# A decoder layer on one core: the first norm's first four blocks turned by VectorE and DRAM transfers, the first pooling group placed later

## The chip, the cores and the metric

The kernel runs on one core of a Trainium2 chip. The metric is the device time of one execution in microseconds (us), lower is better. Three executions of the kernel before took 984.05, 984.94 and 985.39 us (median 984.94). The engines are named as in the profile: PE is TensorE, DVE VectorE, ACT ScalarE, POOL GpSimd, SP the engine that mostly issues transfers.

## The reference

The kernel computes one layer of a decoder for 1024 tokens of width 1024 in float32.

```python
z = h @ w_in[i]                                  # 1024 -> 512 pool | 512 q | 128 k | 128 v
y_pool = pool_mixer(u_pool, w_pool[i], pool_scale[i])   # causal means over 2, 4, 8, 16 tokens, minus the token, one 128x128 map per group
y_attn = sliding_window_attention(q, k, v, attn_sinks[i])  # 8 query heads, 2 kv heads, band of 128, sinks
mix = jnp.concatenate([y_pool, y_attn], axis=-1) @ w_out[i]
h = layer_norm(DEEPNORM_ALPHA * h + mix, ln1_g[i], ln1_b[i])
ff = jnp.square(jax.nn.relu(h @ w_ff1[i])) @ w_ff2[i]      # 1024 -> 4096 -> 1024
h = layer_norm(DEEPNORM_ALPHA * h + ff, ln2_g[i], ln2_b[i])
gate = jax.nn.sigmoid(h @ w_ple_gate[i] + b_ple_gate[i])
h = h + gate * (p[i] @ w_ple[i])
```

## The kernel before, in words

The 1024 tokens are eight blocks of 128; a block is called a token here, as in the code (`n` from 0 to 7), and four of them make a half (`t` = 0 or 1, 512 tokens). Every float32 product is made of three matmuls: each operand is split into a high part (a cast, `high`, L101, on ACT) and the rest (a subtraction, `low`, L106, on DVE or POOL), and `mm3` (L116 to L118) issues high·high, high·low, low·high into one PSUM bank.

The kernel is written as a plain sequence of calls. A scheduler that simulates the engines turns it into one fixed order of instructions for each engine and its queue; each engine then works through its order and waits, where an operand or a buffer is not ready, with everything behind it. So a call that is moved in the text can change the order on all engines for some distance around it. Buffers come from pools by tag, each with a small number of slots: in PSUM the tag `s` has two banks (attention scores, L298 and L299, and the fourth accumulator of `out_left`), `av` one, and further banks hold `pt` (transposes) and `mm` (accumulators).

The stages around the change:

- Projection and attention. `z_tile` makes 128 columns of z for one half (24 matmuls). `attention(n)` makes the scores of a query block in tiles `s`, four per block, two score pairs in each; DVE empties them (L302, into `e`), ACT takes the exponential (L309), DVE scales (L313, L315), PE transposes `e` (L322), ACT and DVE split it (`pp`), and PE multiplies with the values (L327, L328, `av`).
- Pooling. `pool_group(gi, t, o)` (L354 to L388) takes the z tile `o` of one of four groups: ACT copies it (L358), POOL builds the window sums (L366), DVE subtracts (L369), ACT and DVE split the result into `tmp`, PE multiplies with the group's map (`mm<-tmp,wp`), and ACT and DVE scale and split that (L385). There are eight groups, in the order of `steps`, and `pooling(n)` keeps two z tiles ahead of them.
- Mixing. `out_left(t)` makes the left 512 columns of the output projection for four tokens at once, `out_right(n)` the right 512 for one token; `residual` (L457, DVE) adds them onto the input block `hn[n]` and thereby frees the PSUM bank.
- First norm. `norm1(n)` normalises `hn[n]` (L404 to L424 and L121: statistics and two long passes on DVE, one on ACT, one short step on POOL), turns it so that the columns lie on the partitions (`transposed`, L444: eight 128x128 PE transposes per token, four into a bank of tag `pt` and four into `av`), scales the unturned block and stores it (L549, L550, ACT), and splits the two turned halves into X["11"] and X["21"] (ACT casts, DVE subtractions); for tokens 0 to 2 the first is also copied into `pre` (L553).
- The feed-forward stage begins with `early(p)` (L598 to L612), which loads a piece of w_ff1 on SP's queue (L600), splits it, and multiplies it with X["11"] and X["21"] of the first half. In the text the order is out_right(0..3), out_left(1), norm1(0..3), residual of tokens 4 to 7, out_right(4..7), early(0).
- In the tail a similar turning is already done without PE: `flip` (L427 to L436) has DVE transpose 32x32 blocks of a token, writes the result to a DRAM scratch `td` (512 KB) and reads it back in four pieces of 128 KB with the blocks rearranged, all on POOL's queue.

Of the kernel before, what the change touches and what calls it, by code (L numbers as in the profile page):

```python
# [7 lines left out]
F32 = mybir.dt.float32  # L8
# [4 lines left out]
P = 128  # L13
D = 1024
S = 1024
HALF = 512
NT = S // P
NK = D // P
# [52 lines left out]
def layer(ctx, tc, xT, x, pT, w_in, w_pool, pscale, sinks, w_out, ln1, w1, w2, ln2, w_ple, w_gate, bgate, bias, rcount, out):  # L71
# [63 lines left out]


    h_dram = [tc.dram_tile([P, D], F32, name=f"hd{n}") for n in range(NT)]
    t_dram = [tc.dram_tile([P, 4, 2 * P], F32, name=f"td{n}") for n in range(2 * NT)]
    s_dram = [tc.dram_tile([P, 2, HALF], F32, name=f"sd{q}") for q in range(NSUM)]
    g_dram = {t: [tc.dram_tile([P, 2, HALF], F32, name=f"g{t}{i}") for i in range(2)] for t in ("T1", "T2", "T3", "T4")}  # L140
    f_dram = [tc.dram_tile([P, 2, 2, 2, HALF], F32, name=f"fd{q}") for q in range(NQUAD - NKEEP)]
# [32 lines left out]
    def tr_ps():  # L174
        return ps.tile([P, 4, P], F32, tag="pt", bufs=2, name=nm("pt"))
# [15 lines left out]
    def z_tile(c, t, home=None):  # L191
        w = (home or wt)([P, 2, NK, P])
        loads.append(load_split(w[:, 0], w[:, 1], w_in[c], [P, NK, P], nc.vector))
        o = acc_ps()
        for k in range(NK):
            z_mm(o, w, t, k)
        return o
# [146 lines left out]
    steps = [(gi, t) for t in range(2) for gi in (3, 2, 1, 0)]  # L344
    ahead = []

    def pooling(n):
        for _ in range(n):
            while steps and len(ahead) < 2:
                gi, t = steps.pop(0)  # L350
                ahead.append((gi, t, z_tile(6 + gi, t)))
            pool_group(*ahead.pop(0))

    def pool_group(gi, t, o):  # L354
        win = WINDOWS[gi]
# [82 lines left out]
    def tr_av():  # L438
        return ps.tile([P, 4, P], F32, tag="av", bufs=1, name=nm("av"))

    def transposed(y, j, pt):
        for k in range(4):
            kt = 4 * j + k
            nc.tensor.transpose(pt[:, k, :], y[:, kt * P : (kt + 1) * P], ident)  # L444
        return pt
# [54 lines left out]
    keys(1, z_tile(0, 1))  # L500
    attention(2)
    queries(1, 1)
    pooling(1)
    attention(3)
    values(1, z_tile(1, 1))
    pooling(1)
    attention(4)
    pooling(2)
    attention(5)
    pooling(2)  # L510
    attention(6)
    pooling(2)
    left = out_left(0, lambda: stage([P, 2, HALF]), nc.vector)
    with tc.issue_after(loads[-1].ins):
        residual_load(0)
# [10 lines left out]
    def part(shape=(P, 2, 4, P), dt=F32R):  # L526
        return p1.tile(list(shape), dt, tag="ws", bufs=6, name=nm("ws"))
# [10 lines left out]
    def split_to(name, c, src, eng):  # L538
# [2 lines left out]
        high(dh, src)  # L541
        return low(eng, X[name][:, 1, :, cs], src, dh)

    def norm1(n):
        t, c = n // 4, n % 4
        layer_norm(hn[n], gb1)
        a = transposed(hn[n], 0, tr_ps())
        b = transposed(hn[n], 1, tr_av())
        nc.scalar.mul(out=hn[n], in_=hn[n], mul=ALPHA)  # L549
        nc.scalar.dma_start(out=h_dram[n], in_=hn[n])  # L550
        if t == 0:
# [603 lines left out]
```

## Time and profile before

| what | value |
|---|---|
| median of three executions | 984.94 us |
| profiled execution | 984.01 us, its span 982.2 us |
| granted TensorE clock | 1.000 |
| PE busy | 973.8 us, 99% |
| DVE busy | 750.4 us, 76% |
| ACT busy | 470.6 us, 48% |
| POOL busy | 129.5 us, 13% |
| mean DMA rate | 175 GB/s |

The profile is of one execution; its times count from the first instruction, and the execution's own time is longer than this span by 1.8 us. A row of the timeline gives start, duration, engine, line, operation and tiles, and in brackets how long the engine was idle before it and what ended that. A row of the chain gives start, the time that the piece holds the path, engine, tile and line. A row of waits gives who waited for whom, the sum in us, how often, and the longest. Successive matmuls overlap, so a duration of a matmul is longer than its share of the path. PE idles at few places: at the start, at 92.8 and 156.6 us in the attention phase, and in the tail.

### The profile page before, as it was taken

To read this page: it belongs to the slowest core of one execution; us is meant where nothing else is said; L and a number is where in the kernel's file an instruction comes from. 1 tells how busy PE (TensorE), PEld (TensorE's weight loads), DVE (VectorE), ACT (ScalarE), POOL (GpSimd) and SP (SyncE) were. 2 spreads that over 40 slices of the span, in tenths; PEclk is the share of its full clock that TensorE was granted. 3 is DMA by queue.
4 is the path that set the end of the run, shared out by engine and by line. 5 is a ranking of instruction groups with operands and counts; after the bars stand their busy time and mean duration, and the time that the engine had idled before them with its cause. 6 is when DMAs were issued, how large, how long until landed. Compare 5 with 4: busy or idle time off the path is not lost.

```text
span 982.2 us, 12301 instructions
## 1 busy us (share of the span) xinstructions
PE 973.8 (99%) x4474; PEld 809.3 (82%) x4474; DVE 750.4 (76%) x1188; ACT 470.6 (48%) x749; POOL 129.5 (13%) x185
## 2 busy tenths in 40 slices
PE   9999999999999999999999999999999999999998
PEld 7888887888888888888888888888888888878887
DVE  5798888895868876867547666888657699799895
ACT  5676666543475443434444344443434354554341
POOL 0013552020010000110000000100011111203210
PEclk9999999999999999999999999999999999999999
DMA  6512142623152544896264794675788866762741
GB/s 220 183 65 86 44 150 75 219 82 115 69 198 103 197 150 159 298 324 242 78 245 172 278 322 149 150 243 194 207 217 190 223 158 225 252 193 77 257 148 55
DMA packets 48188, 172.13 MB, mean 175 GB/s; under 512 B 6016, under 2 KB 7168, under 8 KB 45312
## 3 DMA queue, kind: packets, MB, share of 16 engines
q1 hardware_dynamic: 35584, 130.05, 38.6%
q0 software_dynamic: 10960, 36.71, 14.6%
q10 hardware_dynamic: 1584, 4.59, 1.2%
q8 instruction: 35, 0.57, 0.2%
q14 instruction: 25, 0.20, 0.1%
HBM read 138.82 MB, written 32.51 MB: 174 GB/s over the span
## 4 chain that ended last, share of the span: by engine, by line
PE 94%; DVE 2%; DMA 2%; issue 1%; ACT 1%; DVEq 0%
PE f L117 21%; PE f L118 21%; PE f L116 21%; PE mm L116 8%; PE mm L118 8%; PE mm L117 8%; DMA ws<-in_w_gate 2%; PE pt L322 1%; PE s L299 1%; PE s L298 1%; PE av L328 1%; PE av L327 1%; DVE w L106 0%; PE s L116 0%; ACT c L101 0%
## 5 line engine op out<-in xcount | busy, mean ns | idle before, releaser
L117 PE MATMUL f<-x,w 128*128 128x512 f32 x448 | 174.0, 389 | 0.4 <-DVE x L106 0.4
L118 PE MATMUL f<-x,w 128*128 128x512 f32 x448 | 173.9, 389 | 0.0
L116 PE MATMUL f<-c,ws 128*128 128x512 f32 (+1 forms) x420 | 162.5, 387 | 0.0
L117 PE MATMUL f<-c,ws 128*128 128x512 f32 (+1 forms) x420 | 162.5, 387 | 0.0
L118 PE MATMUL f<-c,ws 128*128 128x512 f32 (+1 forms) x420 | 161.3, 387 | 0.0
L116 PE MATMUL f<-x,w 128*128 128x512 f32 x448 | 147.1, 389 | 0.1
L101 ACT CAST w<-st 128x1024 fp32r<-128x1024 f32 (+2 forms) x66 | 65.6, 999 | 100.2 <-issue 57.9
L106 DVE TENSOR_TENSOR w<-st,w 128x1024 fp32r<-128x1024 f32 (+2 forms) x66 | 77.5, 1177 | 46.9 <-ACT w L101 46.8
L117 PEld LDWEIGHTS f<-x,w 128*128 128x128 f32 x448 | 84.1, 188 | 18.8 <-DVE x L106 1.1
L116 PEld LDWEIGHTS f<-x,w 128*128 128x128 f32 x448 | 84.0, 188 | 17.9 <-ACT x L101 0.5
L118 PEld LDWEIGHTS f<-x,w 128*128 128x128 f32 x448 | 84.1, 188 | 17.3
L118 PEld LDWEIGHTS f<-c,ws 128*128 128x128 f32 x420 | 78.9, 188 | 16.5 <-DVE ws L106 0.4
L117 PEld LDWEIGHTS f<-c,ws 128*128 128x128 f32 x420 | 78.9, 188 | 16.0
L116 PEld LDWEIGHTS f<-c,ws 128*128 128x128 f32 x420 | 78.9, 188 | 16.0
L106 DVE TENSOR_TENSOR x<-ws,x 128x1024 fp32r<-128x1024 f32 x54 | 65.8, 1219 | 1.5 <-ACT x L101 1.5
L101 ACT CAST ws<-w 128x512 fp32r<-128x512 f32 x60 | 36.9, 622 | 52.0 <-PE f L118 26.5
L106 DVE TENSOR_TENSOR ws<-w,ws 128x512 fp32r<-128x512 f32 x60 | 41.2, 690 | 25.3 <-ACT ws L101 24.6
L101 ACT CAST x<-ws 128x1024 fp32r<-128x1024 f32 x54 | 56.6, 1048 | 7.4 <-DMA ws<-gT 4.0
L101 ACT CAST ws<-st 128x512 fp32r<-128x512 f32 x48 | 29.8, 620 | 62.2 <-DVE st L121 30.8
L116 PE MATMUL mm<-c,w 128*128 128x512 f32 x144 | 56.4, 396 | 0.3 <-ACT w L101 0.3
L118 PE MATMUL mm<-c,w 128*128 128x512 f32 x144 | 56.6, 394 | 0.0
L117 PE MATMUL mm<-c,w 128*128 128x512 f32 x144 | 56.4, 393 | 0.0
(236 smaller groups left out, 1905.5 us busy)
## 6 DMA issues: line engine op xcount, KB each, us to landing
ws<-in_w SPq DMA_DIRECT2D x70, 512.0 KB, 3.8
w<-in_w SPq DMA_DIRECT2D x16, 1024.0 KB, 5.4
c<-fd SPq DMA_DIRECT2D x6, 2048.0 KB, 8.6
fd<-n POOLq DMA_DIRECT2D x20, 512.0 KB, 4.3
ws<-in_w POOLq DMA_DIRECT2D x20, 512.0 KB, 7.6
st<-in_w_in SPq DMA_DIRECT2D x17, 512.0 KB, 3.4
ws<-in_w_gate SPq DMA_DIRECT2D x16, 512.0 KB, 4.6
w<-in_w SPq DMA_DIRECT2D x10, 512.0 KB, 4.0
```

What stands on the lines that cost most here:

```text
L101: nc.scalar.copy(out=dst, in_=src)
L106: return eng.tensor_tensor(out=dst, in0=src, in1=hi.bitcast(F32), op=ALU.subtract)
L116: nc.tensor.matmul(o, ah, bh, start=first, stop=False, skip_group_check=more)
L117: nc.tensor.matmul(o, ah, bl, start=False, stop=False, skip_group_check=more)
L118: nc.tensor.matmul(o, al, bh, start=False, stop=last, skip_group_check=more)
L298: nc.tensor.matmul(s[:, i, dst], ql, kt[:, 0, g, kk : kk + kn], start=True, stop=False)
L299: nc.tensor.matmul(s[:, i, dst], ql, kt[:, 1, g, kk : kk + kn], start=False, stop=True)
L322: nc.tensor.transpose(pt[:, i, :], e[:, i, kb * P : (kb + 1) * P], ident)
L327: nc.tensor.matmul(av, VV[0][:, blk, g], pp[:, 0], start=(kb == lo), stop=False)
L328: nc.tensor.matmul(av, VV[0][:, blk, g], pp[:, 1], start=False, stop=(kb == 1))
```

## The change

There are two parts. The first pooling group (`gi` 3 of half 0), whose z tile is still made behind `queries(1, 1)`, is worked off only behind attention(3) and the z tile of the second half's values; `pooling` is replaced by `project` (make the next z tile) and direct calls of `pool_group`, and the sequence of all later calls stays what it was. And for tokens 0 to 3 `norm1` no longer has PE transposes: `flip_first` has DVE transpose 32x32 blocks of the normalised token into two rows of `pre`, SP writes them to the token's DRAM scratch and reads four pieces back into a tile of tag `ws`, and ACT and DVE make the same copies and splits as before out of that tile in SBUF. Tokens 4 to 7 keep the PE transposes. The argument `False` of `layer_norm` is its default.

```diff
--- before.py
+++ after.py
@@ -135,7 +135,7 @@
 
 
     h_dram = [tc.dram_tile([P, D], F32, name=f"hd{n}") for n in range(NT)]
-    t_dram = [tc.dram_tile([P, 4, 2 * P], F32, name=f"td{n}") for n in range(2 * NT)]
+    t_dram = [tc.dram_tile([4, P, 2 * P] if n < 4 else [P, 4, 2 * P], F32, name=f"td{n}") for n in range(2 * NT)]
     s_dram = [tc.dram_tile([P, 2, HALF], F32, name=f"sd{q}") for q in range(NSUM)]
     g_dram = {t: [tc.dram_tile([P, 2, HALF], F32, name=f"g{t}{i}") for i in range(2)] for t in ("T1", "T2", "T3", "T4")}
     f_dram = [tc.dram_tile([P, 2, 2, 2, HALF], F32, name=f"fd{q}") for q in range(NQUAD - NKEEP)]
@@ -344,12 +344,9 @@
     steps = [(gi, t) for t in range(2) for gi in (3, 2, 1, 0)]
     ahead = []
 
-    def pooling(n):
-        for _ in range(n):
-            while steps and len(ahead) < 2:
-                gi, t = steps.pop(0)
-                ahead.append((gi, t, z_tile(6 + gi, t)))
-            pool_group(*ahead.pop(0))
+    def project():
+        gi, t = steps.pop(0)
+        ahead.append((gi, t, z_tile(6 + gi, t)))
 
     def pool_group(gi, t, o):
         win = WINDOWS[gi]
@@ -500,16 +497,28 @@
     keys(1, z_tile(0, 1))
     attention(2)
     queries(1, 1)
-    pooling(1)
+    project()
+    project()
     attention(3)
-    values(1, z_tile(1, 1))
-    pooling(1)
+    zv = z_tile(1, 1)
+    pool_group(*ahead.pop(0))
+    values(1, zv)
+    project()
+    pool_group(*ahead.pop(0))
     attention(4)
-    pooling(2)
+    project()
+    pool_group(*ahead.pop(0))
+    project()
+    pool_group(*ahead.pop(0))
     attention(5)
-    pooling(2)
+    project()
+    pool_group(*ahead.pop(0))
+    project()
+    pool_group(*ahead.pop(0))
     attention(6)
-    pooling(2)
+    project()
+    pool_group(*ahead.pop(0))
+    pool_group(*ahead.pop(0))
     left = out_left(0, lambda: stage([P, 2, HALF]), nc.vector)
     with tc.issue_after(loads[-1].ins):
         residual_load(0)
@@ -541,11 +550,29 @@
         high(dh, src)
         return low(eng, X[name][:, 1, :, cs], src, dh)
 
+    def flip_first(y, n, t):
+        b, d = pre[:, 2 * (n % 2) : 2 * (n % 2) + 2].rearrange("p a b -> p (a b)"), t_dram[n]
+        nc.vector.transpose(
+            out=b.rearrange("p (q k c) -> p q k c", q=4, k=NK),
+            in_=y.rearrange("p (k q r) -> p q k r", k=NK, q=4),
+        )
+        nc.sync.dma_start(out=d.rearrange("q p e -> p q e"), in_=b.rearrange("p (q e) -> p q e", q=4))
+        for q in range(4):
+            nc.sync.dma_start(
+                out=t[32 * q : 32 * q + 32].rearrange("r (R e) -> r R e", R=4),
+                in_=d[q].rearrange("(R r) e -> r R e", R=4),
+            )
+        tv = t.rearrange("p (R k c) -> p k R c", R=4, k=NK)
+        return tv[:, 0:4], tv[:, 4:8]
+
     def norm1(n):
         t, c = n // 4, n % 4
-        layer_norm(hn[n], gb1)
-        a = transposed(hn[n], 0, tr_ps())
-        b = transposed(hn[n], 1, tr_av())
+        layer_norm(hn[n], gb1, False)
+        if t == 0:
+            a, b = flip_first(hn[n], n, part((P, D), F32))
+        else:
+            a = transposed(hn[n], 0, tr_ps())
+            b = transposed(hn[n], 1, tr_av())
         nc.scalar.mul(out=hn[n], in_=hn[n], mul=ALPHA)
         nc.scalar.dma_start(out=h_dram[n], in_=hn[n])
         if t == 0:
```

The scheduler's order changes at three places that matter here. The first is PE between the end of `out_left(1)` (tile s_342) and `out_right(4)`. Before (pt and av are the transposes of tokens 0 and 1, mm_369 is the accumulator of out_right(4)):

```order
L116 MATMUL s_342_2144<-x7_338_2140,c_197_1303 128x512
L117 MATMUL s_342_2144<-x7_338_2140,c_197_1303 128x512
L118 MATMUL s_342_2144<-x7_338_2140,c_197_1303 128x512
L444 MATMUL pt_355_2281<-ident_61,n_298_1892 128x128 x4
L444 MATMUL av_356_2286<-ident_61,n_298_1892 128x128 x4
L444 MATMUL pt_359_2312<-ident_61,n_299_1894 128x128 x4
L116 MATMUL mm_369_2394<-c_323_2011,c_243_1555 128x512
L117 MATMUL mm_369_2394<-c_323_2011,c_243_1555 128x512
L118 MATMUL mm_369_2394<-c_323_2011,c_243_1555 128x512
```

And after (mm_365 is the accumulator of out_right(4)):

```order
L116 MATMUL s_342_2144<-x7_338_2140,c_197_1303 128x512
L117 MATMUL s_342_2144<-x7_338_2140,c_197_1303 128x512
L118 MATMUL s_342_2144<-x7_338_2140,c_197_1303 128x512
L116 MATMUL mm_365_2382<-c_323_2011,c_243_1555 128x512
L117 MATMUL mm_365_2382<-c_323_2011,c_243_1555 128x512
L118 MATMUL mm_365_2382<-c_323_2011,c_243_1555 128x512
```

Three groups of transposes are gone between the two; the other five, which stood among the products of out_right(4..7), are gone as well.

The second place is DVE from there back to the norm. Before (n_301 is token 3, normalised, n_349 and n_350 are tokens 4 and 5, ws and w are splits of the weights of early(p), sm are small statistics):

```order
L106 TENSOR_TENSOR ws_379_2505<-ws_378_2503,ws_379_2505 128x512
L106 TENSOR_TENSOR ws_380_2508<-ws_378_2503,ws_380_2508 128x512
L419 SCALAR_TENSOR_TENSOR sm_366_2363<-sm_366_2363 128x1
L106 TENSOR_TENSOR ws_390_2568<-ws_389_2566,ws_390_2568 128x512
L106 TENSOR_TENSOR ws_391_2571<-ws_389_2566,ws_391_2571 128x512
L420 TENSOR_SCALAR sm_366_2363<-sm_366_2363 128x1
L421 TENSOR_TENSOR sm_366_2363<-sm_366_2363 128x1
L424 SCALAR_TENSOR_TENSOR n_301_1898<-n_301_1898,sm_366_2363,st_329_2029 128x1024
L106 TENSOR_TENSOR ws_395_2606<-w_394_2604,ws_395_2606 128x512
L106 TENSOR_TENSOR ws_396_2609<-w_394_2604,ws_396_2609 128x512
L121 TENSOR_TENSOR n_301_1898<-n_301_1898,st_330_2030 128x1024
L457 SCALAR_TENSOR_TENSOR n_349_2259<-n_349_2259,mm_339_2141 128x512
```

And after (pre is what the block transposes write, n_300 is token 2, ws_355 and ws_358 are tokens 0 and 1 as they come back from DRAM, c_335 and c_336 are X["11"] and X["21"]; L421 and L454 are the lines that were L424 and L457):

```order
L106 TENSOR_TENSOR c_335_2137<-ws_355_2281,c_335_2137 128x4x128
L106 TENSOR_TENSOR c_336_2138<-ws_355_2281,c_336_2138 128x4x128
L121 TENSOR_TENSOR n_300_1896<-n_300_1896,st_330_2030 128x1024
L417 TENSOR_SCALAR sm_363_2354<-sm_363_2354 128x1
L555 STREAM_TRANSPOSE pre_337_2139<-n_300_1896 128x1024
L418 TENSOR_TENSOR sm_363_2354<-sm_363_2354 128x1
L421 SCALAR_TENSOR_TENSOR n_301_1898<-n_301_1898,sm_363_2354,st_329_2029 128x1024
L121 TENSOR_TENSOR n_301_1898<-n_301_1898,st_330_2030 128x1024
L555 STREAM_TRANSPOSE pre_337_2139<-n_301_1898 128x1024
L106 TENSOR_TENSOR c_335_2137<-ws_358_2309,c_335_2137 128x4x128
L106 TENSOR_TENSOR c_336_2138<-ws_358_2309,c_336_2138 128x4x128
L454 SCALAR_TENSOR_TENSOR n_349_2259<-n_349_2259,mm_339_2141 128x512
```

The weight splits have left this stretch for one behind it; four block transposes (L555, two of them in these rows) and the low parts of tokens 0 and 1 have come into it, ahead of the residual that frees the bank of mm_339. On SP's queue the four reads of token 1 stand behind a load of `w` for the early products, which is issued when its slot is free, and all transfers of the flips stand ahead of the first two loads (`ws`) of early(0) and early(1), which were ahead of the norm before.

The third place is PE ahead of `out_left(0)`, late in the attention phase. Before (pt and e belong to an attention block, s_266 is a score tile, mm_280 the product of a pooling group, s_289 the fourth accumulator of out_left(0)):

```order
L322 MATMUL pt_230_1483<-ident_61,e_225_1456 128x128
L322 MATMUL pt_232_1493<-ident_61,e_225_1456 128x128 x4
L298 MATMUL s_266_1666<-k_100_726,n_129_903 128x256
L299 MATMUL s_266_1666<-k_100_726,n_129_903 128x256
L116 MATMUL mm_280_1750<-tmp_279_1747,wp_122 128x512
L117 MATMUL mm_280_1750<-tmp_279_1747,wp_122 128x512
L118 MATMUL mm_280_1750<-tmp_279_1747,wp_122 128x512
L116 MATMUL s_289_1775<-w_290_1776,c_141_988 128x512
L117 MATMUL s_289_1775<-w_290_1776,c_141_988 128x512
```

And after (mm_275 is a z tile, the dots stand for six more of its matmuls):

```order
L298 MATMUL s_266_1666<-k_100_726,n_129_903 128x256
L299 MATMUL s_266_1666<-k_100_726,n_129_903 128x256
L118 MATMUL mm_275_1714<-c_12_136,w_273_1709 128x512
L116 MATMUL mm_275_1714<-c_13_137,w_273_1709 128x512
L117 MATMUL mm_275_1714<-c_13_137,w_273_1709 128x512
L118 MATMUL mm_275_1714<-c_13_137,w_273_1709 128x512
...
L327 MATMUL av_229_1482<-pp_231_1488,k_29_297 128x512
L116 MATMUL mm_275_1714<-c_13_137,w_273_1709 128x512
L117 MATMUL mm_275_1714<-c_13_137,w_273_1709 128x512
L118 MATMUL mm_275_1714<-c_13_137,w_273_1709 128x512
L116 MATMUL s_289_1775<-w_290_1776,c_165_1121 128x512
```

The tag has two banks, so s_289 takes that of s_265, the score tile ahead of s_266. Between s_265 and s_289 there stand 12 matmuls of 512 columns in the order before and 32 now, with the same transposes and the four of s_266 beside them: a whole z tile has come between. In the same way, behind attention(3)'s second score tile, the z tile of the values now stands: 11 of its matmuls before the third score tile and 13 more before the fourth, where before the four score tiles stood in a row; on DVE the pooling group's subtraction (L369) no longer stands between the first two of them.

## The prediction

> **What bounds the kernel now.** I read the page first: the busy times (part 1) and, from part 4, the shares of the chain of work that ended last.
>
> ```profile
> PE 973.8 (99%) x4474; PEld 809.3 (82%) x4474; DVE 750.4 (76%) x1188; ACT 470.6 (48%) x749; POOL 129.5 (13%) x185
> PE 94%; DVE 2%; DMA 2%; issue 1%; ACT 1%; DVEq 0%
> ```
>
> TensorE is busy for 973.8 of the span of 982.2 us, and 94% of the chain is TensorE's own work. So time is saved in two ways only: by work taken off TensorE, and by waits of TensorE that go, which can be 982.2 − 973.8 = 8.4 us at most. Of the other engines only one question matters: does something that TensorE waits for come later than now? The view of waits, for PE, names the largest of these 8.4 us:
>
> ```profile
> PE pt L393 <- POOL ident masks.py:199: 1.4, 1, 1.4
> PE s L116 <- DVE sm L302: 1.2, 1, 1.2
> PE s L298 <- DVE sm L302: 0.9, 1, 0.9
> ```
>
> The first lies at the start and the change doesn't reach it. The other two lie in the attention phase; both are TensorE waiting for a score bank (tag s, two buffers) that VectorE has not emptied yet. The change touches both places.
>
> **First part: the transposes of tokens 0 to 3.** What leaves TensorE are 32 matmuls of L444, four to a group. Two views price them, the grouped lines and, for 228 to 262 us, the chain:
>
> ```profile
> L444 PE MATMUL pt<-ident,n 128*128 128x128 f32 x32 | 4.8, 272 | 0.0
> ...
> 234.24 0.44 PE pt L444 x4
> ...
> 256.76 0.44 PE av L444 x4
> 257.19 0.24 PE mm L117
> ...
> 259.52 0.23 PE mm L118
> ```
>
> Of one matmul the mean of 272 ns runs from its start to its end, and the next starts before that end. On the path a group of four takes 0.44 us: the matmul behind the last group starts at 257.19, 0.43 us later. There are eight such groups between the first and the last of these rows, so 8 × 0.44 = 3.5 us go. [...]
>
> What comes in their place is off TensorE. For each of the four tokens: one VectorE block transpose, a write of 512 KB to DRAM and four reads of 128 KB on SP's queue, then the same casts as before (ACT's high parts, VectorE's low parts), now out of SBUF. The tail of the kernel does the same flip through POOL's queue, so its rows give the prices (the grouped lines, the table of DMA issues, then the timeline of POOL and of SP):
>
> ```profile
> L429 DVE STREAM_TRANSPOSE n<-pre 128x1024 f32<-128x1024 f32 x4 | 5.0, 1243 | 0.0
> td<-n POOLq DMA_DIRECT2D x8, 512.0 KB, 3.6
> n<-td POOLq DMA_DIRECT2D x32, 128.0 KB, 5.5
> ws<-in_w SPq DMA_DIRECT2D x70, 512.0 KB, 3.8
> 917.55 0.56 POOL L430 DMA_DIRECT2D td<-n  x1
> 926.67 2.21 POOL L432 DMA_DIRECT2D n<-td  x4 [8.56 <-DMA td<-n]
> 219.09 0.33 SPq L600 DMA_DIRECT2D w<-in_w  x1
> ```
>
> A flip takes 1.24 us of VectorE and then 3.6 (write) + 3 × 0.33 (SP's issues) + 5.5 (last read) = 10.1 us of transfer. In the worst row a write keeps its reads waiting for 9.1 us (926.67 − 917.55) in place of 3.6. What would have to hide this, all in the clock of before:
>
> ```profile
> 210.88 1.22 DVE L121 TENSOR_TENSOR n<-n,st 128x1024 f32<-128x1024 f32 x1
> 218.63 1.29 DVE L106 TENSOR_TENSOR ws<-ws,ws 128x512 fp32r<-128x512 f32 x2
> 225.13 1.22 DVE L121 TENSOR_TENSOR n<-n,st 128x1024 f32<-128x1024 f32 x1
> 232.24 1.37 DVE L457 SCALAR_TENSOR_TENSOR n<-n,mm 128x512 f32<-128x512 f32 x2 [5.88 <-PE mm L118]
> 234.72 0.59 ACT L553 COPY pre<-pt 128x512 f32<-128x512 f32 x1 [10.31 <-PE pt L444]
> 235.82 0.69 DVE L106 TENSOR_TENSOR c<-pt,c 128x512 fp32r<-128x512 f32 x1 [0.43 <-ACT c L101]
> ```
>
> These are VectorE's last step of the norm of tokens 1 and 3, a pair of weight splits, the residual of token 4, and the first copies out of the transposes. There are two consumers.
>
> - early(0) needs all four tokens turned. TensorE reaches it at 259.5 now, at 259.5 − 3.5 = 256.0 without the transposes. Token 3 is normalised at 225.13 + 1.22 = 226.4. Ahead of it VectorE gets four transposes (5.0 us) and the low parts of two tokens (4 × 0.69 = 2.8), and loses six weight splits that the order now puts behind (3 × 1.29 = 3.9): 226.4 + 3.9 = 230.3 with its own transpose. With 10.1 of transfer and 3 × 0.6 + 0.7 = 2.5 for ACT's three copies and the last low part it is ready at 242.9. That leaves 13.1 us, more than the worst write takes away (5.5).
> - out_right(4) follows directly on out_left(1) in the new order, at 234.08, where the transposes stand now. It needs the bank that the residual of token 4 frees, and on VectorE that residual now stands behind the low parts of tokens 0 and 1, which wait for their transfers. It has to start by 234.08 − 0.69 = 233.4. By VectorE's own work it can start at 230.3, so 3.1 us are left; VectorE's 5.88 us of idle time ahead of it are what this is paid from. By the transfers: token 1 is turned at 210.88 + 1.22 + 2 × 1.24 = 214.6, its write lands by 218.2, but SP has the load of w (219.09 now, it waits for its slot) ahead of the reads, so they go at 219.4 and land at 219.4 + 1.0 + 5.5 = 225.9; with the copies 228.4. The slack is 5.0. With the worst 9.1 us for both the write and the reads it is 214.6 + 9.1 + 1.0 + 8.6 + 2.5 = 235.8, or 2.4 us late. So this costs between 0 and 2.4 us; I take 0, since the medians leave 3 us or more.
>
> ACT's part is hidden: before the copies of now it sits idle for 10.31 us, and it gets one form of cast for another. SP's twenty new issues are 20 × 0.33 = 6.6 us of its queue; behind them stand the first two weight loads of early(0), which move from before the norm to behind the flips (about 233). They land 3.8 us later, and the splits (two casts on ACT, 1.29 on VectorE for a pair) are done near 240, also ahead of 256.0.
>
> **Second part: the first pooling group.** It moves behind attention(3) and the z tile of the second values. No work is removed; the sum changes only through the two waits. The chain around the first, then around the second:
>
> ```profile
> 91.19 0.09 DVE sm L302
> 91.27 0.61 DVE h L369
> 91.88 0.92 DVE w L106
> ...
> 93.73 0.10 DVE sm L302
> ...
> 93.88 0.39 PE s L298
> ```
>
> ```profile
> 153.97 0.66 DVE c L385
> 154.63 1.17 DVE tmp L106
> 155.79 1.14 DVE w L106
> ...
> 157.66 0.09 DVE sm L302
> ...
> 157.79 0.50 PE s L116
> ```
>
> At 93.88 TensorE runs four score tiles in a row, and the fourth waits for the second one's bank, while VectorE does the group's L369 (0.61) and a weight split (0.92) between them. In the new order 11 matmuls of the z tile stand between the second and the third score tile and 13 more before the fourth; at a step of 0.23 us that is 5.5 us of work to cover the 1.53 us. This wait goes: −0.9. At 157.79 the fourth accumulator of out_left(0) waits for the bank of a score tile, whose emptying (L302) stands on VectorE behind L385, a low part of a pooling group and a weight split (0.66 + 1.17 + 1.14). Between that score tile and the accumulator there are 12 matmuls of 512 columns now and 32 in the new order: 20 × 0.23 = 4.6 us more against a wait of 1.2. It goes too: −1.2. New waits are bounded by the load of VectorE in these stretches of 20 us:
>
> ```profile
> 120.00:140.00 20.00, 20.00 (x109) 16.98 (x108) 16.25 (x41) 13.74 (x29) 11.46 (x15) 1.00 0.42 157
> 140.00:160.00 20.00, 18.79 (x96) 15.43 (x95) 19.14 (x42) 15.36 (x39) 10.31 (x10) 1.00 0.24 80
> ```
>
> VectorE, the third busy column, has 0.9 us free in the second stretch, and the same work has to fit. A wait that reappears elsewhere is between 0 and 2.1 us (all that went); I take 0.4, since only the 0.9 us of idle time in that stretch are missing, and half of it may be found in TensorE's new order.
>
> **The sum.** −3.5 − 0.9 − 1.2 + 0.4 = −5.2 us. The profiled execution took 984.01 us (its span 982.2), so 978.8; the median of the three runs is 984.94, 0.93 above it. From the median: 979.7 us.
>
> **The rivals.**
> - *Only the transposes count.* The attention phase is bound by VectorE and POOL, so the two waits appear at other places. For it: 19.14 of 20 us busy. Against it: the stretch before it has 3.8 us free, and both waits come from the neighbourhood of instructions, which changes. Time: 984.94 − 3.5 = 981.4.
> - *The delayed group bunches.* Its VectorE work (L369 0.61, a low part of 0.69, L385 0.66, together 2.0 us) now falls into the stretch with attention(4) and the second group, which had its own. If TensorE waits for that and for out_right(4)'s bank by the bound of 2.4, the sum is −3.5 − 0.9 + 2.0 + 2.4 = 0.0: 984.9; with the first alone it is −2.4: 982.5. Against it: 120 to 140 has room.
> - *Slower: VectorE blocked in its own queue.* SP is in order, and the load of w ahead of token 1's reads waits for a slot that TensorE frees. Reads that go at R are turned into low parts at R + 6.5 + 2.5; the residual is due at 233.4, so the stall begins at R = 224.4 and each further microsecond costs one. If the slot were the one that TensorE frees last, at the end of out_left(1) (234.08), it is 9.7 us, and the time 984.94 − 3.5 − 2.1 + 9.7 = 989.0. It is slower than before from R = 230.0 on. Against it: this load goes at 219.09 now. [...]
> - That the change doesn't do what it says is excluded by the order: no L444 of tokens 0 to 3 is left on TensorE.
>
> **How the numbers follow.** A measurement of this kernel can tell about 0.2% from no change, which is 2.0 us: faster is below 983.0, slower above 986.9. My forecast (both waits go, the flip is hidden) has 0.54. Only the transposes: 0.26, also faster. The bunched group, at 982.5 to 984.9: 0.14, of which 0.02 still count as faster. Blocked in the queue: 0.06, slower. So faster 0.82, same 0.12, slower 0.06. The range: its low end is 984.94 − 3.5 − 2.1 − 1.2 (if of the rest of the 8.4 us as much again goes as in the larger of the two waits) = 978.1; its high end takes in the rival of the transposes and half of the bunched group, 983.4. What lies outside is the blocked queue and the other half, 0.13, and some below the low end.
>
> **What would show it.** In the profile after: no L444 between 228 and 256, and early(0)'s first product some 5.6 us earlier than 259.5 (right, if 253 to 255). PE's waits without the rows of L302 at 0.9 and 1.2 (first part of the second term). The residual of token 4 on VectorE released by TensorE, not by ACT or by a DMA: if its idle time ends on a cast of a flipped token, VectorE was blocked, and PE's waits then have a row of mm L116 on that residual. If the time is near 981.4 and rows of L302 stand at new places, the rival of the transposes is right. If PE's busy time falls by clearly less or more than 3.5 us, the price of a transpose was wrong.

## The result and the profile after

The changed kernel takes 980.81 us (median of five runs, 979.77 to 981.71) against 984.94 us; the ratio is 0.9959, its 95% interval 0.9947 to 0.9970. That is 4.1 us less, and 1.1 us more than the 979.7 forecast. The profiled execution of the changed kernel took 981.71 us (its span 979.9), the longest of the five. The page after, busy times and the chain's shares by engine:

```profile
PE 971.5 (99%) x4442; PEld 804.7 (82%) x4442; DVE 755.7 (77%) x1192; ACT 470.5 (48%) x749; POOL 128.8 (13%) x185
PE 83%; DVE 11%; DMA 3%; issue 2%; ACT 1%; ACTq 0%; DVEq 0%
```

TensorE has 32 instructions less. But its share of the chain has fallen from 94 to 83%, and VectorE and the transfers have taken what it lost: the chain's rows place this at 140 to 163 us, up to the wait on `pp` in the list below, and at 793 to 927 us, where it hangs on a load of `gT`. The share also varies by itself: a second profile of before has 87%. PE's waits, after:

```profile
PE pt L390 <- POOL ident masks.py:199: 1.4, 1, 1.4
PE f L117 <- DVE x L106: 0.8, 2, 0.4
PE f L118 <- DVE ws L106: 0.7, 1, 0.7
PE mm L116 <- ACT c L101: 0.6, 2, 0.4
PE s L117 <- DVE w L106: 0.5, 1, 0.5
PE mm L116 <- ACT w L101: 0.3, 1, 0.3
PE av L328 <- DVE pp L106: 0.2, 1, 0.2
```

The two waits of before on L302 are gone. In the attention phase `s L117` (0.5) and `av L328` (0.2) are new; the two rows of `f` lie in the tail, and both waits on `ACT c L101` in the start-up. To see which stage gained what, one counts along TensorE's own order: each kernel issues 1354 products of a low with a high part (L118), and, but for the attention phase, where some change places, it issues them in the same sequence. So the start of the n-th (from 0) can be set against the n-th of the other. Four of those starts, after: n = 250 (in out_left(1)), 400, 1150 and the last:

```profile
224.76 0.39 PE L118 MATMUL mm<-x,c 128*128 128x512 f32 x1
331.01 0.39 PE L118 MATMUL f<-c,ws 128*128 128x512 f32 x1
841.13 0.39 PE L118 MATMUL f<-x,w 128*128 128x512 f32 x1
975.77 0.28 PE L118 MATMUL f<-c,c 128*128 128x256 f32 x1
```

In before they stand at 225.01, 334.56, 844.68 and 977.84. With n = 25 (24.12 and 25.12) as the end of the start-up, the stages of nine profiles compare as follows; each is the difference of two such starts, less the same difference in the first profile of before:

| profile | start-up, to n=25 | attention, 25-250 | norm and early products, 250-400 | feed-forward, 400-1150 | tail, 1150 to the end |
|---|---|---|---|---|---|
| before | 24.12 | 200.89 | 109.55 | 510.13 | 133.15 |
| before, again | +0.32 | +0.06 | 0.00 | +0.41 | +0.45 |
| changed | +1.00 | −1.25 | −3.29 | −0.01 | +1.49 |
| changed, again | +0.82 | −1.22 | −3.73 | −0.03 | +1.41 |
| only the pooling group | −0.36 | −1.23 | 0.00 | −0.01 | +0.25 |
| only the flip | −0.02 | +0.03 | −3.75 | −0.01 | +2.76 |
| only the flip, 4 small transfers | −0.47 | +0.05 | −3.36 | 0.00 | +1.00 |
| no turning | +0.16 | −1.21 | −3.75 | +0.03 | +0.83 |
| no turning, 4 small transfers | +0.23 | −1.25 | −3.75 | +0.03 | +3.20 |

The middle of the kernel repeats to a few hundredths, but for two places of 0.4 us (−3.29 and −3.36, both looked at below). The start-up and the tail don't.

### The profile page after: what moved, and what is told of

It is laid out like the page before. It is cut to its first block, busy times and chain, and to the rows that moved or that the text cites. A ratio compares the mean times of both kernels' runs of the same rounds, so it can differ in the third digit from the quotient of the medians.

```text
span 979.9 us, 12263 instructions
## 1 busy us (share of the span) xinstructions
PE 971.5 (99%) x4442; PEld 804.7 (82%) x4442; DVE 755.7 (77%) x1192; ACT 470.5 (48%) x749; POOL 128.8 (13%) x185
## 4 chain that ended last, share of the span: by engine, by line
PE 83%; DVE 11%; DMA 3%; issue 2%; ACT 1%; ACTq 0%; DVEq 0%
PE f L118 18%; PE f L116 18%; PE f L117 18%; PE mm L116 8%; PE mm L118 8%; PE mm L117 8%; DMA ws<-in_w_gate 1%; DVE w L106 1%; PE pt L322 1%; DVE n L121 1%; DMA ws<-gT 1%; DVE c L106 1%; DVE x L106 1%; PE s L299 1%; DVE n L426 1%
## 5 line engine op out<-in xcount | busy, mean ns | idle before, releaser
L117 PE MATMUL f<-x,w 128*128 128x512 f32 x448 | 174.1, 390 | 0.8 <-DVE x L106 0.8
L118 PE MATMUL f<-x,w 128*128 128x512 f32 x448 | 173.8, 389 | 0.0
L117 PE MATMUL f<-c,ws 128*128 128x512 f32 (+1 forms) x420 | 162.5, 387 | 0.0
L118 PE MATMUL f<-c,ws 128*128 128x512 f32 (+1 forms) x420 | 161.5, 388 | 0.7 <-DVE ws L106 0.7
L101 ACT CAST w<-st 128x1024 fp32r<-128x1024 f32 (+2 forms) x66 | 65.8, 998 | 102.2 <-issue 62.8
L117 PEld LDWEIGHTS f<-x,w 128*128 128x128 f32 x448 | 84.1, 188 | 19.4 <-DVE x L106 1.9
L118 PEld LDWEIGHTS f<-x,w 128*128 128x128 f32 x448 | 84.1, 188 | 17.4
L118 PEld LDWEIGHTS f<-c,ws 128*128 128x128 f32 x420 | 78.9, 188 | 17.6 <-DVE ws L106 1.5
L117 PEld LDWEIGHTS f<-c,ws 128*128 128x128 f32 x420 | 78.8, 188 | 16.1
L101 ACT CAST ws<-w 128x512 fp32r<-128x512 f32 x60 | 37.0, 622 | 48.3 <-PE f L118 28.0
L101 ACT CAST ws<-st 128x512 fp32r<-128x512 f32 x48 | 29.8, 620 | 61.6 <-DVE st L121 31.1
L101 ACT CAST x<-ws 128x1024 fp32r<-128x1024 f32 x54 | 56.6, 1048 | 4.6 <-PE f L118 3.5
L118 PE MATMUL mm<-c,w 128*128 128x512 f32 x144 | 56.8, 395 | 0.0
L117 PE MATMUL mm<-c,w 128*128 128x512 f32 x144 | 56.6, 394 | 0.0
```

Source lines behind the costliest of these rows:

```text
L101: nc.scalar.copy(out=dst, in_=src)
L117: nc.tensor.matmul(o, ah, bl, start=False, stop=False, skip_group_check=more)
L118: nc.tensor.matmul(o, al, bh, start=False, stop=last, skip_group_check=more)
```

## The experiments

**The two parts apart.** The first run keeps the transposes and moves only the pooling group; the second turns tokens 0 to 3 the new way and leaves the pooling groups where they were.

```diff
     queries(1, 1)
-    pooling(1)
+    project()
+    project()
     attention(3)
-    values(1, z_tile(1, 1))
-    pooling(1)
+    zv = z_tile(1, 1)
+    pool_group(*ahead.pop(0))
+    values(1, zv)
...
```

> Only the first pooling group is moved; the 32 transposes stay on TensorE. In the profile after, the stretch from 100 to 225 us gained 1.3 us. If the two parts add up, this kernel takes 984.9 - 1.3 = 983.6 us, its PE waits have no row of L298 at 0.9 and a new one of about 0.5 on DVE w L106 at out_left(0). Rival (only the transposes count): 984.9, no change. Rival (the group bunches behind attention(4)): slower than before by up to 2 us.

Measured: 983.45 us, ratio 0.9985 (0.9977 to 0.9994), as expected. PE's waits in the attention phase of this run:

```profile
PE s L117 <- DVE w L106: 0.5, 1, 0.5
PE av L328 <- DVE pp L106: 0.2, 1, 0.2
```

> Only the turning of tokens 0 to 3 is changed; the pooling groups stand as before. If the flip is hidden, 32 transposes at 0.11 us are all that goes: 984.9 - 3.5 = 981.4 us, the waits of L298 and L116 on DVE sm L302 (0.9 and 1.2) stay. Rival (the flip costs part of what it saves, on VectorE or behind the residual of token 4): 982.5 or more, with a new PE wait of mm L116 near 233 us.

```diff
-        a = transposed(hn[n], 0, tr_ps())
-        b = transposed(hn[n], 1, tr_av())
+        if t == 0:
+            a, b = flip_first(hn[n], n, part((P, D), F32))
+        else:
+            a = transposed(hn[n], 0, tr_ps())
+            b = transposed(hn[n], 1, tr_av())
```

Measured: 982.82 us, ratio 0.9981 (0.9971 to 0.9991). The rival's number, but not for its reason. Its waits near the norm are none; of the attention phase the two of before are left, and the largest new one is in the tail:

```profile
PE s L116 <- DVE sm L302: 1.2, 1, 1.2
PE f L118 <- DVE ws L106: 1.1, 1, 1.1
PE s L298 <- DVE sm L302: 0.9, 1, 0.9
```

The flip gains 3.75 us in its stage; 2.76 of them are lost again behind 841 us in the profiled execution. The two parts add up stage by stage (−1.23 and −3.75 against −1.22 and −3.73 together).

**Does the flip cost anything where it stands?** In the changed kernel the splits now read the normalised token itself, so nothing is turned and nothing transferred; the computation differs from the reference's in that operand.

```diff
-            a, b = flip_first(hn[n], n, part((P, D), F32))
+            a, b = (hn[n][:, j * HALF : (j + 1) * HALF].rearrange("p (k t) -> p k t", k=4) for j in range(2))
```

> The changed kernel with no turning at all for tokens 0 to 3: the splits read the normalised token itself, so the first feed-forward operand holds unturned blocks. No block transpose, no write, no reads. If the flip is hidden, this takes as long as the changed kernel, 980.8 within 0.5 us. Rival (the flip's VectorE work or transfers cost): faster than the changed kernel by what it costs, 979.5 or less for a cost of 1.3 us or more.

Measured: 980.03 us, ratio 0.9958 (0.9944 to 0.9971). The stage from 250 to 400 is −3.75, as with the flip (−3.75 and −3.73): in these two profiles the flip is hidden to 0.02 us. The time lies between the two expectations. The 0.8 to 1.4 us between the medians lie elsewhere: in the profiles in the start-up, in the tail and in one wait that comes next.

**The changed kernel once more.**

> The changed kernel once more, to see which waits of its first profile come back. Theory: the 1.0 us at the start and the 1.5 us of waits from 840 us on follow from landing times of loads and vary, so they differ in this profile, while the stretch from 20 to 260 us repeats within 0.3 us; 980.8 us. Rival: they belong to the change and come back in place and size.

Measured: 981.46 us, ratio 0.9963 (0.9950 to 0.9976). The middle repeats, but for 0.44 us in the early products. The first profile loses 0.3 of them at 267.67, where the weights of a product are loaded only when ACT has copied an earlier product out of its bank, and the rest at the transposes behind it:

```profile
267.67 0.19 PEld L116 LDWEIGHTS mm<-c,ws 128*128 128x128 f32 x1 [0.40 <-ACT pre L631]
```

Why ACT was later there in this one profile stays open. The start-up and the tail repeat as well (+0.82 and +1.41), which the theory did not expect.

**Before once more.**

> The kernel before once more, for a second profile of it. From 20 to 845 us it should repeat within 0.1 us. Theory (the start and the tail vary from run to run whatever the kernel): the tail, from the 1150th low-high product to the end, differs from the first profile's by up to 1.5 us. Rival (the tail is longer because TensorE reaches it earlier, or because of the flips): the tail repeats the first profile within 0.3 us.

Measured: 985.26 us in its one execution. Its tail is 0.45 us longer than the first's, inside the 1.5 us that the theory allows, but smaller than the difference to the changed kernel.

**How near the flip is to being late.** Two kernels send each turned token once more through DRAM. In the first the scheduler is free; in the second the residuals of tokens 4 to 7 are kept behind token 1's low parts, as the changed kernel has them.

```diff
+        for w in (t_dram[n + 4].rearrange("p q e -> p (q e)"),):
+            nc.sync.dma_start(out=w, in_=b)
+            nc.sync.dma_start(out=b, in_=w)
         nc.sync.dma_start(out=d.rearrange("q p e -> p q e"), in_=b.rearrange("p (q e) -> p q e", q=4))
```

> The changed kernel with one more round trip through DRAM in each of the four flips (the turned token is written, read back and written again). Each token arrives some 6 to 8 us later. The scheduler now puts the residuals of tokens 4 to 7 ahead of token 1's low parts on VectorE. Theory (the only tight place is the residual behind those low parts, early(0) has over 6 us): no new wait at 233 us, and at most some at early(0) near 255: 981 to 984 us. Rival (the transfers themselves set the time): 6 us or more slower than the changed kernel, 987.

Measured: 986.94 us, ratio 1.002 (1.0004 to 1.0036): a miss, and the rival's number. The profiled execution was the fastest of its ten (981.79), so it shows only the beginning of the loss: from 250 to 400 it is −0.95 where the changed kernel has −3.73, with one new wait:

```profile
PE mm L116 <- ACT ws L101: 2.0, 2, 1.5
```

These are the first weights of the early products, whose loads stand behind the flips in SP's queue. What the slower executions wait for was not recorded.

```diff
-    residual_left(1, os)
+    with tc.issue_after(turned[1].ins):
+        residual_left(1, os)
```

> The same with the longer flips, but the residuals of tokens 4 to 7 are kept behind token 1's low parts on VectorE, as the changed kernel has them. Theory (VectorE's own queue blocks): token 1 is ready some 6 to 9 us after 231.5, out_right(4) waits that long for its bank, with a PE wait of mm L116 on DVE in the 230s: 6 to 9 us slower than the changed kernel, 987 to 990. Rival (something else frees the bank, or PE has other work): as the run with the longer flips alone.

Measured: 992.46 us, ratio 1.0084 (1.0068 to 1.0100), at the place that was named and with more than was expected. PE's largest wait, VectorE's rows ahead of it, and the stretches of the wait and behind it (the column 0.68, 0.57 is the granted clock, which is 1.00 before and after):

```profile
PE mm L116 <- DVE n L454: 9.7, 1, 9.7
```

```profile
240.88 1.29 DVE L106 TENSOR_TENSOR c<-ws,c 128x512 fp32r<-128x512 f32 x2 [4.00 <-ACT c L101]
242.09 1.87 DVE L454 SCALAR_TENSOR_TENSOR n<-n,mm 128x512 f32<-128x512 f32 x3
```

```profile
232.00:242.60 10.60, 1.09 (x5) 0.56 (x3) 2.96 (x4) 2.71 (x4) 0.00 (x0) 0.68 0.90 320
242.60:246.60 4.00, 3.77 (x10) 3.04 (x11) 2.57 (x5) 0.64 (x2) 0.00 (x0) 0.57 0.82 249
```

VectorE waits for ACT, which waits for token 1; the residual behind it has long had its input (TensorE's last product ahead of the wait starts at 232.70), and TensorE waits for the residual's bank. That is the stall of the prediction's slower rival. Counted from the 250th low-high product (223.86 here, 224.76 in the changed kernel), the residual starts 10.0 us later than there; 0.2 us were left there (below), and TensorE waits 9.7. So here each microsecond of lateness cost one, and some 1.6 us came on top while the granted clock was low (last section).

**All eight tokens flipped.** First in the same way, with a block buffer of tag `n` for tokens 4 to 7:

```diff
-        if t == 0:
-            a, b = flip_first(hn[n], n, part((P, D), F32))
-        else:
-            a = transposed(hn[n], 0, tr_ps())
-            b = transposed(hn[n], 1, tr_av())
+        a, b = flip_first(hn[n], n, part((P, D), F32))
```

> Tokens 4 to 7 are turned by VectorE and DRAM as well; their 32 transposes go too, with a block buffer of tag n. If a group of four costs TensorE 0.44 us there as well and the flips are hidden beside the early products, the stretch from 255 to 320 us is 3.5 to 3.8 us shorter and the time is 977.4. Rival (between the early products the four splits per token and the buffers of tag ws stand in the way): new PE waits on the split operands T1 to T4 behind 300 us, 981 or slower.

Measured: 990.55 us, ratio 1.0067 (1.0050 to 1.0083): slower, as the rival said, but the waits are on other operands than it named. PE's two largest waits, and SP's queue ahead of the first:

```profile
PE mm L116 <- ACT ws L101: 4.4, 1, 4.4
PE mm L116 <- ACT pre L627: 4.4, 2, 3.7
```

```profile
236.48 0.43 SPq L623 DMA_DIRECT2D ws<-in_w  x1
251.43 0.38 SPq L559 DMA_DIRECT2D td<-n  x1
254.28 1.92 SPq L561 DMA_DIRECT2D ws<-td  x4
256.30 0.36 SPq L623 DMA_DIRECT2D ws<-in_w  x1
```

The second load of early weights goes at 256.30, right behind the last read of token 4's flip (254.28 + 1.92), and that flip could not be issued before its token was normalised and turned, at 251.43. TensorE waits for what follows that load. The second kernel uses POOL's queue for tokens 4 to 7 and reads them back into their own tile, once the scaled copy is stored (new function, the first lines):

```diff
+    def flip_later(y, n):
+        b, d = nat([P, D]), t_dram[n]
+        nc.vector.transpose(
...
+        nc.gpsimd.dma_start(out=d.rearrange("q p e -> p q e"), in_=b.rearrange("p (q e) -> p q e", q=4))
+        nc.scalar.mul(out=y, in_=y, mul=ALPHA)
+        nc.scalar.dma_start(out=h_dram[n], in_=y)
...
```

> Tokens 4 to 7 are flipped too, but through POOL's queue and back into the token's own tile, so that neither SP's weight loads nor the buffers of tag ws are touched. Theory (what cost 4.4 + 4.4 us when all eight tokens were flipped was the weights' loads and their buffers, not the flip): the waits on ACT ws L101 and pre are gone, the 32 transposes go with 3.7 us, 977.3 us. Rival (the turned tokens come too late for T1 to T4, or VectorE is full between 255 and 345 us): waits of f L116 to L118 on x or c behind 345 us, 981 or slower.

Measured: 1010.63 us, ratio 1.0262 (1.0245 to 1.0279); the theory is wrong. The waits:

```profile
PE mm L116 <- ACT t L637: 12.5, 3, 10.1
PE f L116 <- ACT c L101: 7.2, 1, 7.2
PE f L116 <- ACT ws L101: 5.1, 2, 4.4
```

The longest comes about so, on POOL and then on ACT:

```profile
299.63 2.22 POOL L578 DMA_DIRECT2D n<-td  x4 [7.97 <-DMA hd<-n]
```

```profile
304.13 0.62 ACT L601 COPY t<-n 128x512 f32<-128x512 f32 x1 [7.45 <-DMA n<-td]
...
305.18 1.07 ACT L637 ACTIVATE t<-mm 128x512 f32<-128x512 f32 x2
```

The reads wait for the store of the scaled copy, ACT waits for the reads, and behind ACT's copy stands L637, which empties the bank that the next early product needs. The last token's split (`c`) is then 7.2 us late for the next stage. Beside the early products neither of the two flips tried here is hidden.

**The wait that came in at out_left(0).** The low parts of its weights go to POOL.

```diff
-    left = out_left(0, lambda: stage([P, 2, HALF]), nc.vector)
+    left = out_left(0, lambda: stage([P, 2, HALF]), nc.gpsimd)
```

> The changed kernel with the low parts of out_left(0)'s weights on POOL in place of VectorE (four passes of 128x1024). Theory (the wait of 0.5 us on DVE w L106 near 160 us, and the 0.6 us around it, are VectorE's full queue): both go, the stretch from the 175th to the 225th low-high product is about 1 us shorter, 980.0 us. Rival (POOL, which takes about 2.7 us for such a pass, delivers later than VectorE): a wait of s L116 to L118 on POOL w L106 in the same place, 981.5 or slower.

Measured: 985.43 us, ratio 1.0014 (1.0003 to 1.0026). The rival's sign, but another wait than it named: the one on `w` (0.5) is gone, and TensorE now waits longest for the one bank of `av`, which VectorE's `y` empties. The rival's 2.7 us for a pass is an estimate: two passes of 128x512, of which POOL's take 1.29 to 1.46 us in the changed kernel's profile. Here POOL is busy for 135.7 us in place of 128.8, or 6.9 us longer for the four passes. The profiled execution was the slowest of twelve (988.62).

```profile
PE av L327 <- DVE y L331: 3.0, 1, 3.0
```

**What the tail depends on.** In the traces of before and after, the 251 and 271 transfers of SP and ACT take completion semaphores in turn, eight of them, with 31 to 34 transfers on each. The flips add 20 transfers (SP has 240 and 260), so each later one has the semaphore four places on: in the traces all 38 that SP issues behind 840 us have it, in the same order. The first load of `gT` in the program's own listing, before and after (the digit behind DMAHW is the semaphore's place among the eight, 5 and 1; the trace has the load at 911.32 on semaphore 107 and at 908.22 on 102, places 5 and 1 of 100, 102, 103, 105, 106, 107, 108, 110):

```
L1004 DMA ws_7380<-gT_104 128x1024 [waits DMAHW5_49,DVE_49]
L1031 DMA ws_7368<-gT_104 128x1024 [waits DMAHW1_49,DVE_49]
```

Four transfers of 1 KB more undo the shift in the kernel with only the flip, and make it in the kernel with no turning (there with `h_dram[3]` as their source, and with that kernel's own order on all engines).

```diff
+    for q in range(4):
+        nc.sync.dma_start(out=t_dram[4][0:1, q], in_=t_dram[3][q, 0:1])
     residual_left(1, os)
```

> The kernel with only the flip (982.8 us) and four transfers of 1 KB more on SP's queue behind the last flip. The flips add 20 transfers, and the semaphores of SP's transfers go round in eights, so every later transfer has another one (shifted by 4); with 24 they are those of before again. Rival (that shift is what lengthens the tail): the stretch from the 1150th low-high product to the end is within 0.5 us of the kernel before, and the time is 981.2. Theory (the tail's transfers land differently from run to run): the tail is 0 to 3 us longer, as with the flip alone, and the time stays at 982 to 983.

Measured: 981.9 us, ratio 0.9977 (0.9966 to 0.9988), with the tail at +1.00 (+2.76 without them). The time is between the two expectations, and the tail is inside the theory's range. In this profile 0.4 us are lost beside the norm, and that is the flip: the residual of token 4, behind the low parts of token 1, ends at 233.90, and TensorE, which by its step of 0.23 us would have come to the bank at 233.67, starts at 233.96:

```profile
233.22 0.68 DVE L457 SCALAR_TENSOR_TENSOR n<-n,mm 128x512 f32<-128x512 f32 x1
233.96 0.50 PE L116 MATMUL mm<-c,c 128*128 128x512 f32 x1
```

> The kernel with no turning for tokens 0 to 3 and four transfers of 1 KB on SP's queue behind the norm; the order of all engines is otherwise that of the run with no turning, and every later transfer of SP has the semaphore that it has in the changed kernel (shifted by 4) in place of that of before. Rival (the shift lengthens the tail): the tail is 1.4 us or more longer than before's first profile and the time is 981.3, 1.2 us above the run with no turning. Theory (the shift does nothing, the tail's transfers land differently from run to run): 980.0, as with no turning.

Measured: 981.31 us, ratio 0.9965 (0.9952 to 0.9979), the rival's number; the tail is +3.20 (+0.83 without them). The chain of the changed kernel shows what the tail's late wait hangs on, a load of `gT`; then VectorE at that place in this run, and in the one with no turning:

```profile
912.76 10.23 DMA ws<-gT
```

```profile
921.40 1.23 DVE L106 TENSOR_TENSOR w<-ws,w 128x1024 fp32r<-128x1024 f32 x1 [6.39 <-ACT w L101]
```

```profile
918.62 1.23 DVE L106 TENSOR_TENSOR w<-ws,w 128x1024 fp32r<-128x1024 f32 x1 [4.78 <-ACT w L101]
```

Over all profiles the tail takes 132.90 to 134.15 us in the six with the semaphores of before (mean 133.5) and 133.72 to 136.81 in the eight with the shift (mean 135.2). That goes with the medians: the pooling group alone and no turning keep what the middle gains (1.5 of 1.2, 4.9 of 5.0 us), the changed kernel and the flip alone lose 0.9 to 1.7 us of it. With the four small transfers, the flip loses 0.7 without the shift and no turning 1.4 with it. The two groups also overlap, each pair of intervals does too, and why a semaphore's number should matter was not found. The traces show a second difference, on POOL's queue. In the three profiles of kernels that turn all eight tokens on TensorE, a write of `td` shortly before these loads takes 4.8 to 5.1 us to land, and the reads behind it go at the time of the second load of `gT` or after it. In the other eleven the write takes 3.0 to 3.1 us and the reads go 1.7 to 1.9 us ahead of that load, which then takes 6.7 to 9.3 us to land in place of 3.2 to 3.6. The reads in the first profile of before and after (the second load of `gT` goes at 915.00 and 911.90):

```profile
915.26 2.21 POOL L432 DMA_DIRECT2D n<-td  x4 [5.31 <-DMA td<-n]
910.08 2.21 POOL L429 DMA_DIRECT2D n<-td  x4 [3.22 <-ACT t L993]
```

So once the first four tokens are not turned on TensorE, the tail's transfers come in another order, with the shift and without it. But the three of the eleven that have no shift still have tails of 132.90 to 134.15 us. It is open whether the shift lengthens the tail, or what else decides how late these loads land. That the tail can be this long without a flip is shown by the last run: it has none, its TensorE arrives when its twin's does (839.94 against 839.91), and its tail is 2.4 us longer. The changed kernel with the shift undone was not tried.

## Why the prediction was right, and where it was off

- **The transposes.** Forecast −3.5, measured −3.75 in the stage (−3.29 in the one profile with 0.44 us of waits). The term was 0.2 us small: why eight groups cost 0.47 and not the 0.44 of their rows was not looked into. The priced path step (0.109 us for one transpose), not the 0.27 us of its duration, was the right one. Priced by that duration, 32 × 0.272 = 8.7 us, the term would have been 5 too much. TensorE's busy time fell by only 2.3 us in the whole span, which the forecast had named as a sign against this price; but between the 250th and the 400th product it fell by 3.3 (3.7 in the second profile), and the start-up, the attention phase and the tail put 1.0 back. early(0)'s first product starts at 255.59 in place of 259.58, just outside the 253 to 255 that were named, because the start-up of this profile is 1.0 us longer.
- **The flip is hidden.** Right, and shown by the run with no turning. But the margin was not the 3 to 5 us of the text. VectorE, ACT, SP and TensorE around it, after:

```profile
227.01 1.25 DVE L555 STREAM_TRANSPOSE pre<-n 128x1024 f32<-128x1024 f32 x1
231.75 1.29 DVE L106 TENSOR_TENSOR c<-ws,c 128x512 fp32r<-128x512 f32 x2 [3.50 <-ACT c L101]
232.96 1.27 DVE L454 SCALAR_TENSOR_TENSOR n<-n,mm 128x512 f32<-128x512 f32 x2
```

```profile
230.57 0.62 ACT L580 COPY pre<-ws 128x512 f32<-128x512 f32 x1 [5.19 <-DMA ws<-td]
```

```profile
221.32 0.36 SPq L627 DMA_DIRECT2D w<-in_w  x1
221.77 2.37 SPq L561 DMA_DIRECT2D ws<-td  x4
```

```profile
233.60 0.39 PE L118 MATMUL s<-x,c 128*128 128x512 f32 x1
233.82 0.39 PE L116 MATMUL mm<-c,c 128*128 128x512 f32 x1
```

VectorE's own work ended at 227.01 + 1.25 = 228.3, earlier than the 230.3 forecast. The transfers were the late part: by them the residual was to start at 228.4, and it started at 232.96. Of these 4.6 us, 2.4 came before the reads: the load of `w` ahead of them waited for a slot that TensorE freed later than before (SP waits 2.9 us for it), so it went at 221.32 and not at 219.09, and the reads at 221.77 and not at 219.4. SP's issues took 0.4 us more than the 1.0 of the sum. The last read landed 7.2 us after its issue in place of 5.5, at 230.4, which made 1.8; ACT's first copy then started at 230.57. VectorE's idle time did end on ACT's cast of a flipped token, the sign of a blocked queue, but TensorE did not feel it: the first of the two residuals ended at 233.64, and TensorE took its bank at 233.82 without a gap. So 0.2 us were left, 0.4 in the second profile of this kernel and in the one with only the flip, and with the four small transfers they were missing. Two steps failed, then: the time of the load of `w`, which was read off the kernel before, and the price of the reads, which was the median of the tail's, while here the load of `w` (issued at 221.32) and a store of ACT (issued at 222.06) were under way with them (whether that made them slow was not tried apart). The first is the slower rival's own mechanism, in small. The upper end of this term is also too low: with 9.1 us for the reads, as the text says, and not the 8.6 of the sum, it is 2.9 us and not 2.4. That nothing was lost here, within a stated range of 0 to 2.4 us, is luck.
- **The pooling group.** Forecast −2.1 + 0.4, measured −1.25. Both waits on L302 went, as worked out. The 0.4 us for new ones should have been 0.85. They come where the forecast looked for them, in VectorE's load in the 20 us ahead of out_left(0). That load, and VectorE's order there, after:

```profile
140.00:160.00 20.00, 20.00 (x106) 16.92 (x104) 19.45 (x47) 16.58 (x38) 11.28 (x12) 1.00 0.15 54
```

```profile
157.67 1.96 DVE L315 TENSOR_SCALAR e<-e,sm 128x256 f32<-128x256 f32 x4
159.55 1.21 DVE L106 TENSOR_TENSOR w<-st,w 128x1024 fp32r<-128x1024 f32 x1
```

```profile
160.82 0.49 PE L117 MATMUL s<-w,c 128*128 128x512 f32 x1 [0.53 <-DVE w L106]
```

VectorE is busier than before (19.45 of 20 us), and the weights' low part now is what TensorE waits for. The rival "only the transposes count" is out: the pooling group alone makes the kernel faster, by 0.6 to 2.3 per mille.
- **The sum.** The middle gave −1.25 − 3.75 = −5.0, the forecast said −5.2. What reached the end is −4.1 in the first series and −3.4 in the second. The step that failed is that a gain on TensorE was taken to reach the end whole, with the chain as TensorE's throughout. Before's own chain has 2% DMA and 2% VectorE, most of them between 829 and 869 us, in the tail. In both profiles of the changed kernel the tail is 1.4 to 1.5 us longer, and the cause of that is open, as said above. The start-up is 0.8 to 1.0 us longer as well; no other kernel of the table shows that, although five of them have one part of the change or both, and its cause is open too. The middle alone came within 0.2 us of the forecast, and that in part by luck: the transposes gave 0.25 us more than forecast and the pooling group 0.45 less.
- **Which engine should turn.** Here TensorE is the engine without room (busy for 99% of the span): taking its path away gained 3.75 us, and with no turning at all the stage gained no more. With all eight tokens, in the two ways tried, the kernel was slower than with TensorE's transposes for the last four (990.55 and 1010.63 us against 980.81).

## What to carry to other kernels

Here one engine was busy 99% of the span, and work moved from it to others was worth its step on that engine's path (3.75 us for the 32 transposes) and not its duration (8.7 us). It was paid for in order: in the queue of each engine that it passed, somebody else's work stood behind its wait, as VectorE's residual did, for which TensorE waited 9.7 us once the tokens came later. So list what is queued behind the new wait and when that is due; here 0.2 us were left (in another profile 0.4 were missing), one more round trip in that order cost 11 us, and the same edit for the next four tokens made the kernel slower. Compare stages by counting along the busy engine's own instructions in several profiles: it tells a gain of a few tenths in one stage from a tail that varies by three microseconds.

## What the runs showed of the hardware

After the wait of 9.7 us TensorE's granted clock was low for a while. In that kernel, the one with the blocked residual, TensorE stood still from 233.1 to 242.8; of its next seven products the first then took 0.59 us and the others 0.43 each, in place of 0.23, and the granted clock was 0.57 from 242.6 to 246.6. That is 0.4 + 6 × 0.2 = 1.6 us on top of the wait of 9.7; the two together, 11.3, are the stage's difference to the changed kernel's second profile (7.65 + 3.73 = 11.4). About half the rate (0.43 us for a product) lasted for 3.2 us, from 242.83 to 246.0; from 246.6 to 256 the granted clock was 1.00. The waits of 1.2 us and less in the kernels before and after show no such effect: in before, with waits of 0.9 us up to 93.88 and 1.2 us up to 157.79, the granted clock was 1.00 from 92 to 96 and from 158 to 162, and in the changed kernel, with one of 0.5 us up to 160.82, from 157 to 161 and from 161 to 165.
